# Step 2 of each batch of SSM parameters, moved from one unit behind step 1 to 1.6 units behind, with its TensorE work queued behind that unit's op 7

## The chip, the cores and the metric

The kernel runs on one core of one Trainium2 chip. The metric is the device time of one execution, in microseconds (us). The engines of the core each work through a queue of their own: TensorE (PE, and PEld for its weight loads), VectorE (DVE), ScalarE (ACT), GpSimd (POOL), and SyncE (SP), which here issues all transfers.

## What is computed

One layer of a decoder, for a prompt of 1024 tokens and 8 samples of 4 tokens (1056 columns in all): a SwiGLU feed-forward half, a mixing block (windowed attention beside a diagonal state-space model, the SSM), and a second feed-forward half. Cut to what the change touches:

```python
def swiglu(x, w1, w3, w2):
    return (jax.nn.silu(x @ w1) * (x @ w3)) @ w2

def trunk_layer(x, ...):
    x = x + 0.5 * swiglu(rms_norm(x, p['ffn1_norm']), p['ffn1_w1'], p['ffn1_w3'], p['ffn1_w2'])
    ...
    y_ssm, new_re, new_im = s5_scan(u, s_re, s_im, a_re, a_im, log_dt, b_re, b_im, c_re, c_im, d)
```

`s5_scan` needs, from its parameters alone (not from x), discretised matrices for 32 groups of channels. The kernel works these out in 8 batches of 4 groups, while the first feed-forward half runs.

## The kernel before, in words

The first feed-forward half has 22 blocks of hidden columns (NFF = 22). Blocks 0 and 1 are multiplied plainly; blocks 2 to 21 go through `up`, one **unit** each. A unit makes the products with w1 and w3 by seven block products (a Winograd-like scheme), the **ops**, in the order 4, 3, 1, 2, 5, 7, 6 (`OPS`). An op has 24 matmuls on TensorE: two column halves, four row blocks, and three passes (high x high, high x low, low x high parts of fp32 operands); a unit has 168. All matmuls of products are recorded by one line of the helper `passes` (L197). The results lie in PSUM tiles P (three buffers of two banks); ops 4, 3, 1 and 6 open a new one. ScalarE and VectorE empty them into the tile e: for op 7 an add (L378), a Silu on ScalarE, and a product with op 2's result (L380), after which the tile of ops 4 and 2 is free.

Weights come four transfers to a unit (L292), are combined on VectorE (ws), and split by ScalarE (cast wh, L308) and VectorE (wl) into eight buffers each, so one op more than a unit. Tiles of 1056 columns share a pool T of 34 buffers. In `up`, 28 of them hold the operands X (seven ops, two halves, high and low); e takes one per unit, and each batch of parameters two, ta and tb.

The SSM parameters of a batch come from the generator `params_b`, in two steps divided by its `yield` (L553). **Step 1** loads "bc" into tb (L528), then GpSimd alone computes: bb and ca into tb, ba and e_ into ta (line L80 for all of it). **Step 2** stores e_ (L554), transposes ba on TensorE (four, "ptr", L559), copies the result with ScalarE to mt (L560) and stores it; copies ca and bb to c2 and b2 (L568, L569), reorders c2 to cp (L573); multiplies b2 by c2 on TensorE (eight matmuls "pk", L580); copies that to kt (L583); spreads kt over tz with eight small transfers (L593), casts it to tp (L595) and stores it. The tiles of step 2 share a pool of four buffers, and "ptr" and "pk" share two PSUM banks (sm).

`hook(f)` is called at the end of unit f. For odd f from 5 to 19 it starts step 1 of batch b = (f - 5) / 2; for even f from 6 to 20 it runs step 2. That fixes the order in which the program is traced, not the order in the engines' queues: the framework plans each queue ahead with its own timing model, takes at any moment the instruction that it has as ready, and prefers the one traced earlier. `issue_after(ins)` adds an edge that holds the instructions traced in the block, on the engine of `ins` only, behind `ins` in that engine's queue; the other engines' instructions are held by their data and buffers alone.

After unit 21 the down projection `down` begins: it loads hr (L396), splits it (cast hh on ScalarE, L398), loads w2a, and multiplies into tiles p.

Of the kernel before, what the change touches and what calls it, by code (L numbers as in the profile page):

```python
# [34 lines left out]
NB = 8  # L35
# [7 lines left out]
def body(tc, I, O):  # L43
    nc = tc.nc
    V, S, Pl, PE = nc.vector, nc.scalar, nc.gpsimd, nc.tensor
    dma = nc.sync.dma_start
    mark = {}
    es = ExitStack()
    with es:
# [32 lines left out]
        def mul(o, a, b, e=V):  # L82
            tt(o, a, b, ALU.mult, e)

        def add(o, a, b, e=V):
            tt(o, a, b, ALU.add, e)

        def sub(o, a, b, e=V):
            tt(o, a, b, ALU.subtract, e)
# [10 lines left out]
        def act(o, a, f, **kw):  # L100
            S.activation(o, a, f, **kw)
# [7 lines left out]
        def TT(name, dt=F32):  # L109
            return big(Tp, "T", name, dt)  # L110
# [5 lines left out]
        def SQ(name, dt=F32, w=C):  # L116
            return sq_p.tile([128, H], dt, tag="sq", name=name)[:, 0:w]
# [35 lines left out]
        def load_consts():  # L153
            dma(vec[:, ARE:], I["vec"][:, ARE:])
            dma(ident, I["ident"])
            dma(mask, I["mask"])
            dma(dvec, I["dvec"])
# [35 lines left out]
        def passes(ps, w, x, first, last, **kw):  # L193

            (h, l), (xh, xl) = w, x
            for i, (a, b) in enumerate(((h, xh), (h, xl), (l, xh))):
                PE.matmul(ps, a, b, start=first and i == 0, stop=last and i == 2, **kw)  # L197

        def gemm_to(ps, wks, xs, cols):
            n = len(wks)  # L200
            for k, ((wu, kb), x) in enumerate(zip(wks, xs)):
                passes(ps, blk(wu, kb), [t[:, cols] for t in x], k == 0, k == n - 1)
# [85 lines left out]
        def wload(s1, s3):  # L288
            r1, r3 = (wr_p.tile([128, 8, 128], F32, tag="wr", name="wr") for _ in range(2))
            a11, a12, a21, a22 = r1[:, 0:4], r1[:, 4:8], r3[:, 0:4], r3[:, 4:8]  # L290
            for a_, src in ((a22, s3[:, 4:8]), (a11, s1[:, 0:4]), (a21, s3[:, 0:4]), (a12, s1[:, 4:8])):
                dma(a_, src)  # L292
            return a11, a12, a21, a22

        def wprep(raw):

            a11, a12, a21, a22 = raw
            W = {}
            for op in OPS:
                if op in RAW:  # L300
                    s = a11 if op == 3 else a22
                else:
                    p, q, f, o = {1: (a11, a22, add, None), 5: (a11, a12, add, None), 2: (a21, a22, add, None),
                                  7: (a12, a22, sub, a12), 6: (a21, a11, sub, a21)}[op]
                    s = ws_p.tile([128, 4, 128], F32, tag="ws", name="ws") if o is None else o
                    f(s, p, q)
                h, l = w4()
                S.copy(h, s)  # L308
                sub(l, s, f32(h))
                W[op] = h, l  # L310
            return W
# [3 lines left out]
        def products(W, X, first):  # L315

            P = {}

            def one(op, j):
                b = BANK[op]  # L320
                for k in range(4):
                    passes(P[b][:, j, 0:J], [t[:, k, :] for t in W[op]], [t[:, k, :] for t in X[op, j]],
                           k == 0 and op in OPENS, k == 3, skip_group_check=op not in OPENS)

            both = slice(0, 2)
            if first:
                for op in OPENS[:3]:
                    P[BANK[op]] = bank("pp", f"P{BANK[op]}")
                for j in range(2):
                    for op in OPS[:6]:  # L330
                        one(op, j)
                        yield op, slice(j, j + 1), P[BANK[op]][:, :, 0:J]
                ops = OPS[6:]
            else:
                ops = OPS
            for op in ops:
                if op in OPENS:
                    P[BANK[op]] = bank("pp", f"P{BANK[op]}")
                for j in range(2):
                    one(op, j)  # L340
                yield op, both, P[BANK[op]][:, :, 0:J]

        def plain(f, j, wu, X, hid):

            P = [bank("pp", f"Q{i}") for i in range(2)]
            e = SQ("e", w=H).rearrange("p (b c) -> p b c", b=2)
            for b in range(2):
                for w_, p in zip(wu, P):
                    for k in range(KD):
                        passes(p[:, b, 0:J], blk(w_, k), [t[:, k % 4, :] for t in X[k // 4, b, j]], k == 0, k == KD - 1)  # L350
                act(e[:, b], P[0][:, b, 0:J], AF.Silu)
                mul(e[:, b], e[:, b], P[1][:, b, 0:J])
                yield
            dma(hj(hid[f], j), e)

        def up(w1, w3, X, hid, f0, hook=None):

            for f in range(f0, NFF):
                W = wprep(wload(w1[f], w3[f]))
                e = TT("e")  # L360
                q_, g_ = (e[:, i * H:i * H + H].rearrange("p (j c) -> p j c", j=2) for i in range(2))
                a_ = SQ("a1", w=H).rearrange("p (j c) -> p j c", j=2)
                for op, js, p_ in products(W, X, f == f0):
                    q, g, a1, p = (t[:, js, :] for t in (q_, g_, a_, p_))
                    if op == 4:
                        S.copy(q, p)
                    elif op == 3:
                        add(q, q, p)
                    elif op == 1:
                        add(g, q, p)  # L370
                    elif op == 5:
                        act(a1, p, AF.Silu)
                        sub(q, q, p)
                    elif op == 2:
                        c21 = p_
                        sub(g, g, p)
                    elif op == 7:
                        mark["up"] = V.tensor_tensor(out=q, in0=q, in1=p, op=ALU.add).ins  # L378
                        act(q, q, AF.Silu)
                        mul(q, q, c21[:, js, :])  # L380
                        dma(hid[f, :, 0:H].rearrange("p (j c) -> p j c", j=2)[:, js, :], q)
                    else:
                        add(g, g, p)
                        mul(g, g, a1)
                        mark["hid"] = dma(hid[f, :, H:T], e[:, H:T]).ins
                if hook:
                    hook(f)

        def down(w, hid, xd_, x, groups):

# [206 lines left out]

        todo = []

        def hook(f):  # L600

            if f == 2:
                with tc.issue_after(mark["hid"]):
                    load_consts()
                with tc.issue_after(mark["up"]):
                    params()
            elif 4 < f < 5 + 2 * NB:
                if f % 2:
                    todo.append(params_b((f - 5) // 2))
                next(todo[-1], None)  # L610


        hid = dr.tile([NFF, 128, T], F32, name="hid")
# [27 lines left out]
        def sums(B, b):  # L641
            ps = SM("ss")[:, 0:J]
            for a in range(2):
                for i in range(2):
                    s = SQ("sq", w=H).rearrange("p (k c) -> p k c", k=2)
                    act(s, B[a, b][:, 2 * i:2 * i + 2, :], AF.Square)
                    for kk in range(2):
                        PE.matmul(ps, f32(ones), s[:, kk, :], start=a + i + kk == 0, stop=a == 1 and i + kk == 2)
            return ps
# [14 lines left out]
        ps = sums(B[0], 0)  # L664
# [22 lines left out]
        for _ in cmb:  # L687
            pass
        up(I["w1a"], I["w3a"], X, hid, 2, hook)
        banks(mm=(4, 1), sm=(4, 1))  # L690
        x = []
# [594 lines left out]
        for _ in combos(B[1], X, 1):  # L1286
            pass
        up(I["w1b"], I["w3b"], X, hid, 2)
        banks(mm=(4, 1), sm=(4, 1))
        x = []  # L1290
# [127 lines left out]
```

## Time and profile before

| | us |
|---|---|
| time, median of 3 runs | 2186.34 (2185.17 to 2187.98) |
| the profiled execution, its own time | 2187.48 |
| its span, first to last instruction | 2185.7 |
| TensorE busy | 2097.5 (96%) |
| VectorE busy | 1409.7 (64%) |
| ScalarE busy | 751.6 (34%) |
| GpSimd busy | 368.7 (17%) |

The profile is one execution. Busy time is the time in which an engine has an instruction running; TensorE's matmuls are pipelined, one of 264 columns shows 0.28 us and the next begins 0.12 us after it. A mark such as [1.64 <-POOL ta L80] in a timeline says that the engine was idle for 1.64 us before the instruction, and that a write of ta by GpSimd at line 80 ended the wait. [...]

### The profile page before, as it was taken

What the parts mean: (1) busy time and instruction counts of PE and PEld (TensorE: products, weight loads), DVE (VectorE), ACT (ScalarE), POOL (GpSimd) and SP (SyncE); (2) the same over time, 40 slices, a digit from 0 to 9 for tenths busy, and PEclk for the clock granted to TensorE, in tenths of its full rate; (3) what the DMA queues carried; (4) which work ended last, traced back from release to release, by engine and by line L of the source; (5) the groups of instructions that cost most, each with busy time, mean ns of one, the idle gap of its engine ahead of it and who ended that gap; (6) DMA issues with size and microseconds to landing.
All of it is one profiled execution on the core that took longest, in us unless ns stands there. A gap on an engine that the chain in (4) does not pass through costs nothing.

```text
span 2185.7 us, 38056 instructions
## 1 busy us (share of the span) xinstructions
PE 2097.5 (96%) x15009; PEld 2064.6 (94%) x15009; DVE 1409.7 (64%) x2580; ACT 751.6 (34%) x1435; POOL 368.7 (17%) x759
## 2 busy tenths in 40 slices
PE   7999999999999999999899799988999999999999
PEld 7999998999999999999899699988999999999999
DVE  5876566655554375757988856778666666565534
ACT  5433343434221152235455543344322222332210
POOL 0017777565000032324200200000000000000000
PEclk8999999999999999999999799999999999999999
DMA  4122322333632234642222264331222212273212
GB/s 157 43 93 83 108 95 82 108 100 120 245 133 59 63 118 159 206 123 68 76 84 93 77 241 153 129 104 40 82 66 88 86 64 86 76 248 118 92 38 80
DMA packets 132947, 234.40 MB, mean 107 GB/s; under 512 B 25936, under 2 KB 62608, under 8 KB 132752
## 3 DMA queue, kind: packets, MB, share of 16 engines
q1 hardware_dynamic: 132768, 231.97, 31.9%
q8 instruction: 118, 1.93, 0.4%
q14 instruction: 61, 0.50, 0.1%
HBM read 164.98 MB, written 64.06 MB: 105 GB/s over the span
## 4 chain that ended last, share of the span: by engine, by line
PE 73%; DVE 7%; POOL 3%; issue 2%; DMA 1%; SPq 1%; ACT 1%; DVEq 0%; POOLq 0%; ACTq 0%
PE p L197 26%; PE P L197 26%; PE pj L197 10%; PE pm L197 4%; POOL tb L80 2%; PE Q L197 2%; PE pg L197 1%; DVE raw L80 1%; POOL ta L80 1%; DVE wl L80 1%; SPq L593 1%; PE po L1016 1%; DVE Xl L80 0%; PE pt L1001 0%; PE sc L975 0%
## 5 line engine op out<-in xcount | busy, mean ns | idle before, releaser
L197 PE MATMUL P<-Xh,wh 128*128 128x264 f32 x2240 | 643.2, 287 | 12.2 <-DVE e L80 7.1
L197 PE MATMUL P<-Xl,wh 128*128 128x264 f32 x2240 | 640.8, 286 | 0.0
L197 PE MATMUL P<-Xh,wl 128*128 128x264 f32 x2240 | 638.4, 285 | 0.0
L197 PEld LDWEIGHTS P<-Xh,wh 128*128 128x128 f32 x2240 | 426.4, 190 | 16.9 <-DVE e L80 6.2
L197 PEld LDWEIGHTS P<-Xh,wl 128*128 128x128 f32 x2240 | 426.6, 190 | 0.0
L197 PEld LDWEIGHTS P<-Xl,wh 128*128 128x128 f32 x2240 | 426.1, 190 | 0.0
L197 PE MATMUL p<-hh,wh 128*128 128x352 f32 x1056 | 340.4, 323 | 5.2 <-DVE x L92 3.4
L197 PE MATMUL p<-hh,wl 128*128 128x352 f32 x1056 | 340.5, 322 | 0.0
L197 PE MATMUL p<-hl,wh 128*128 128x352 f32 x1056 | 340.2, 322 | 0.0
L80 DVE TENSOR_TENSOR wl<-wr,wh 128x512 fp32r<-128x512 f32 (+1 forms) x360 | 246.2, 685 | 115.9 <-ACT wh L308 85.8
L92 DVE SCALAR_TENSOR_TENSOR x<-p,x 128x352 f32<-128x352 f32 x288 | 150.3, 523 | 246.8 <-PE p L197 243.7
L185 ACT CAST wh<-wr 128x512 fp32r<-128x512 f32 (+1 forms) x200 | 120.1, 603 | 460.9 <-PE p L197 331.0
L80 DVE TENSOR_TENSOR e<-e,P 128x528 f32<-128x528 f32 (+1 forms) x250 | 169.8, 680 | 158.2 <-PE P L197 128.1
L197 PE MATMUL pj<-xh,wh 128*128 128x352 f32 x624 | 204.3, 327 | 6.5 <-DVE gt L80 5.4
L197 PEld LDWEIGHTS p<-hh,wh 128*128 128x128 f32 x1056 | 198.3, 188 | 6.5 <-DVE x L92 4.3
L197 PE MATMUL pj<-xl,wh 128*128 128x352 f32 x624 | 203.2, 326 | 0.0
L197 PE MATMUL pj<-xh,wl 128*128 128x352 f32 x624 | 202.7, 325 | 0.0
L197 PEld LDWEIGHTS p<-hl,wh 128*128 128x128 f32 x1056 | 198.7, 188 | 0.0
L197 PEld LDWEIGHTS p<-hh,wl 128*128 128x128 f32 x1056 | 198.5, 188 | 0.0
L308 ACT CAST wh<-wr 128x512 fp32r<-128x512 f32 x160 | 99.5, 622 | 266.2 <-PE P L197 225.9
L308 ACT CAST wh<-ws 128x512 fp32r<-128x512 f32 x120 | 74.5, 622 | 208.9 <-PE P L197 203.0
L197 PEld LDWEIGHTS pj<-xh,wh 128*128 128x128 f32 x624 | 118.6, 190 | 7.9 <-DVE gt L80 5.9
(692 smaller groups left out, 3481.8 us busy)
## 6 DMA issues: line engine op xcount, KB each, us to landing
hr<-hid SPq DMA_DIRECT2D x44, 528.0 KB
hid<-e SPq DMA_DIRECT2D x86, 264.0 KB
wr<-in_w_in SPq DMA_DIRECT2D x26, 512.0 KB
wr<-in_w3a SPq DMA_DIRECT2D x40, 256.0 KB
wr<-in_w1a SPq DMA_DIRECT2D x40, 256.0 KB
wr<-in_w2a SPq DMA_DIRECT2D x40, 256.0 KB
wr<-in_w3b SPq DMA_DIRECT2D x40, 256.0 KB
wr<-in_w1b SPq DMA_DIRECT2D x40, 256.0 KB
```

Of the source, the lines that this page charges most:

```text
L80: e.tensor_tensor(out=o, in0=a, in1=b, op=op)
L92: V.scalar_tensor_tensor(out=o, in0=a, scalar=s, in1=b, op0=op0, op1=op1)
L185: S.copy(h[:, 0:m, :], r[:, i:i + m, :])
L197: PE.matmul(ps, a, b, start=first and i == 0, stop=last and i == 2, **kw)
L308: S.copy(h, s)
L593: dma(tv[:, j, :, j * 16:128], ktg[:, :, 0:(8 - j) * 16])
L1016: PE.matmul(po[:, 0:256], Vs[blk // 4][:, blk % 4, m // 2, :], P[:, a_, kb * 256:kb * 256 + 256], start=i == 0, stop=i == 2 * nk - 1)
```

## The change

Step 1 stays at the end of the odd units. Step 2 of a batch is traced no longer at the end of the unit after step 1, but a unit later, inside unit f + 2, right after op 7's results are taken over, and inside an order edge: `mark["pe"]` is the last matmul traced so far, that of op 7, and the TensorE instructions of step 2 (ptr and pk) stand behind it in TensorE's queue. Batch 0 has step 1 at the end of unit 5 and step 2 in unit 7; batch 7 has step 1 at the end of unit 19 and step 2 in unit 21, the last. Within a unit in which both happen, the older batch's step 2 is traced first.

```diff
             for i, (a, b) in enumerate(((h, xh), (h, xl), (l, xh))):
-                PE.matmul(ps, a, b, start=first and i == 0, stop=last and i == 2, **kw)
+                mark["pe"] = PE.matmul(ps, a, b, start=first and i == 0, stop=last and i == 2, **kw).ins
...
                         dma(hid[f, :, 0:H].rearrange("p (j c) -> p j c", j=2)[:, js, :], q)
+                        if hook:
+                            hook(f, False)
...
                 if hook:
-                    hook(f)
+                    hook(f, True)
...
-        def hook(f):
-
+        def hook(f, end):
+
+            if not end:
+                if f > 5 and f % 2:
+                    with tc.issue_after(mark["pe"]):
+                        next(todo.pop(), None)
+                return
             if f == 2:
...
-            elif 4 < f < 5 + 2 * NB:
-                if f % 2:
-                    todo.append(params_b((f - 5) // 2))
-                next(todo[-1], None)
+            elif f > 4 and f % 2 and f < 5 + 2 * NB:
+                todo.append(params_b((f - 5) // 2))
+                next(todo[-1])
```

## Rows read from the trace of the kernel before

**Rows 1.** The page's first part: engine, busy us, share, instructions.

```profile
PE 2097.5 (96%) x15009; PEld 2064.6 (94%) x15009; DVE 1409.7 (64%) x2580; ACT 751.6 (34%) x1435; POOL 368.7 (17%) x759
```

**Rows 2.** Waits of TensorE, 60 to 560 us: line, releaser, total, times, longest.

```profile
PE ptr L559 <- POOL ta L80: 17.5, 12, 2.0
```

**Rows 3.** Timeline of TensorE: start, duration, line, output from inputs, wait.

```profile
265.36 0.83 PE L559 MATMUL ptr<-ident,ta 128*128 128x128 f32 x3
267.82 0.48 PE L559 MATMUL ptr<-ident,ta 128*128 128x128 f32 x1 [1.64 <-POOL ta L80]
267.95 0.57 PE L197 MATMUL P<-Xh,wh 128*128 128x264 f32 x1
...
289.99 0.62 PE L580 MATMUL pk<-c,b 128*16 128x128 f32 x8
```

**Rows 4.** Timeline of GpSimd, batch 2: first, last of ba, last of e_.

```profile
256.49 0.44 POOL L80 TENSOR_TENSOR tb<-tb,par 128x32 f32<-128x32 f32 x2 [11.11 <-issue]
...
267.31 0.45 POOL L80 TENSOR_TENSOR ta<-tb 128x128 f32<-128x128 f32 x1
...
290.56 0.46 POOL L80 TENSOR_TENSOR ta<-tb 128x128 f32<-128x128 f32 x1
```

**Rows 5.** Windows, ptr to next product: length, busy, clock; sum of batches 1-7.

```profile
177.48:177.83 0.35, 0.35 (x6) 0.35 (x5) 0.15 (x1) 0.22 (x1) 0.27 (x2) 1.00 0.64 228
...
354.56:360.21 5.65, 1.05 (x6) 0.43 (x5) 4.47 (x6) 0.99 (x2) 5.18 (x9) 0.98 0.33 107
...
sum 23.83, PE 5.98 PEld 2.80 DVE 14.56 ACT 6.44 POOL 21.69; mean PE 0.85 PEld 0.40 DVE 2.08 ACT 0.92 POOL 3.10
```

**Rows 6.** Windows, the seven units from behind pk to ptr: their sum.

```profile
sum 143.40, PE 143.40 PEld 143.40 DVE 94.53 ACT 50.32 POOL 58.98; mean PE 20.49 PEld 20.49 DVE 13.51 ACT 7.19 POOL 8.43
```

**Rows 7.** Windows, the seven units from behind ptr to pk: two, and sum.

```profile
222.27:244.32 22.05, 22.05 (x169) 21.91 (x169) 12.71 (x18) 9.35 (x23) 19.39 (x52) 0.92 0.19 67
...
313.00:333.52 20.52, 20.52 (x169) 20.38 (x169) 12.33 (x18) 9.24 (x23) 18.10 (x48) 1.00 0.25 78
...
sum 152.32, PE 152.32 PEld 151.35 DVE 83.83 ACT 65.21 POOL 132.88; mean PE 21.76 PEld 21.62 DVE 11.98 ACT 9.32 POOL 18.98
```

**Rows 8.** Timeline of SP, batch 1's tz and batch 2's in_bc.

```profile
251.84 2.49 SPq L593 DMA_DIRECT2D tz<-kt  x4
254.38 0.58 SPq L528 DMA_DIRECT2D tb<-in_bc  x1
```

**Rows 9.** Waits of SP's queue, 60 to 560 us.

```profile
SPq L554 <- POOL ta L80: 109.1, 8, 15.2
```

**Rows 10.** Timeline of TensorE and ScalarE at the seam to the down projection.

```profile
544.93 0.36 PE L197 MATMUL P<-Xh,wh 128*128 128x264 f32 x1 [1.69 <-DVE e L80]
...
548.95 0.40 PE L197 MATMUL p<-hh,wh 128*128 128x352 f32 x1 [0.89 <-DVE e L80]
...
541.20 1.08 ACT L398 CAST hh<-hr 128x1056 fp32r<-128x1056 f32 x1 [3.17 <-DMA hr<-hid]
...
542.70 0.60 ACT L101 ACTIVATE a<-P 128x528 f32<-128x528 f32 x1
```

**Rows 11.** Tiles mt, c2, b2, cp: ns min/median/max, first and last start.

```profile
L560 ACT COPY mt<-ptr x16: 364/372/376, 178.1 to 500.4; 128x256 f32<-128x256 f32 x16
...
L568 ACT COPY c<-tb x32: 428/433/438, 180.9 to 507.0; 64x288 f32<-64x288 f32 x32
...
L569 ACT COPY b<-tb x32: 211/215/219, 181.2 to 505.7; 64x32 f32<-64x32 f32 x32
...
L573 ACT COPY cp<-c x32: 407/414/426, 184.6 to 508.5; 128x128 f32<-128x128 f32 x32
```

**Rows 12.** Timeline of ScalarE and TensorE behind ptr, batches 0 and 2.

```profile
182.50 0.65 ACT L101 ACTIVATE e<-e 128x528 f32<-128x528 f32 x1
...
183.94 0.39 PE L197 MATMUL P<-Xh,wh 128*128 128x264 f32 x1
...
273.90 0.62 ACT L308 CAST wh<-wr 128x512 fp32r<-128x512 f32 x1
```

## Prediction

> **What bounds the kernel now.** The page comes first: TensorE is busy 96% of the span [rows 1]. So only what makes TensorE wait, or lowers its clock, can give time. The change touches the first up-projection alone, about 98 to 543 us, so the waits of that stretch come next. There the largest wait of TensorE is for the transposes "ptr" (L559), and what ends it is GpSimd writing "ta" [rows 2]. The timeline of TensorE shows the place. Each group of four transposes stands in its queue between op 7 and op 6 of a unit. I counted the products: 168, one unit, lie between each ptr group and the eight matmuls "pk" (L580), and 168 again up to the next ptr; the last 24 products, op 6 of unit 21, stand alone at 544.93 us [rows 3, 10]. Of batch 2, three transposes run at 265.36 and the fourth waits until 267.82 [rows 3]. The data it waits for left GpSimd at 267.31 + 0.45 us, in a chain that had begun only at 256.49 and runs on to 291 [rows 4].
>
> So step 1 is too late for step 2, although the program puts step 2 one unit later. Counting units back from the end, ptr of batch b stands behind op 7 of unit 5+2b, ahead of the place where the program traces it (end of unit 6+2b): the planner took it earlier, as soon as it thought it ready. That is the fault the change is aimed at.
>
> **What the waits cost.** I measured the eight stretches from the first transpose of a batch to the next product. Batch 0 did not wait: 0.35 us. Batches 1 to 7 took 23.83 us together [rows 5]. What can go is 23.83 - 7 x 0.35 = 21.4 us. (The waits list has 17.5 us; it leaves out the start-up of a matmul after each wait.)
>
> Behind that comes a second cost. The unit before each ptr group, from pk to ptr, takes 20.49 us at a granted clock of 1.00, in all seven cases, sum 143.40 us [rows 6]. The unit behind each ptr group holds the same 168 products, and the seven of them take 152.32 us. [...] Difference: 8.9 us. Together 30.3 us are there to win, 1.4% of the time.
>
> **The change, part by part.**
> *The record of the last matmul* (L197) adds no instruction: nothing.
> *Step 1* stays at the end of unit 5+2b; it is only traced after the previous batch's step 2 instead of being followed by it. *Step 2* of batch b moves from the end of unit 6+2b to op 7 of unit 7+2b, and its 12 TensorE instructions get an order edge behind the last product of that op 7. ptr so goes two units later in TensorE's queue than it stands now, 2 x 20.49 + 0.9 (ptr and pk) = 41.9 us. It is now at most 5.65 us too early [rows 5], so the data is there some 36 us ahead. The 21.4 us go, and the 8.9 us of low clock with them. What is late next on that data is nothing on TensorE: GpSimd needs 34.5 us for a batch (256.49 to 291.0) [rows 4], against 41.9 us for two units.
>
> *SP's queue.* in_bc, which starts step 1, stands behind eight tz transfers of the batch before [rows 8]; with step 2 later these come a unit further on, so step 1 starts up to 5 us earlier: a gain only for slack. The store of "ta" (L554) is not held by the edge. It waits for GpSimd 109.1 us over the eight batches already [rows 9], and the weight loads behind it wait too; TensorE does not feel it, as the eight wh/wl buffers hold a unit of weights (20.5 us). If two units take 41.9 us instead of 45.7 and GpSimd still 34.5, that cover shrinks by about 4 us. I cost it at nothing; without cover it would be those 4 us per batch.
>
> *ptr and pk themselves* are as many as before: nothing.
>
> *pk's new place* is the unknown. Its operands c2 and b2 are copied by ScalarE out of "tb", and the planner will have it ready shortly after ptr, no longer a unit later. mt copies 2 x 0.37, then 4 x 0.43 and 4 x 0.22 = 2.6 us [rows 11]; with 0.3 us from ptr to the first copy and perhaps a Silu of 0.65, ready 3.6 to 4.3 us after ptr. If pk stands behind op 6, TensorE arrives 0.35 + 24 x 0.122 = 3.3 us after ptr, so it waits 0.3 to 1.1 us; if it stands some products further on, or the copies run before ptr (their data is ready long before), it waits nothing. No case of such a wait is in the trace (pk at 289.99 ran at once [rows 3]). The nearest row is batch 0, where the Silu of op 7 came late behind the copies, at 182.50, and op 3 at 183.94 lost about 0.2 us, with no loss of clock [rows 12]. I take 0.5 us x 8 = 4.0 us; bounds 0 and 1.1 x 8 = 8.8. A gain is excluded, since the pk instructions only ever add their own run.
>
> *Batch 7 at the seam.* Its ptr moves from 497.41 to behind op 7 of unit 21, at 543 us, where the down projection begins and TensorE already waits (1.69 us and 0.89 us), because ScalarE, in its order, sits on the cast hh until the transfer hr has landed [rows 10]. ScalarE gets the whole of step 2 there: the 3.3 us above, 4 cp copies 1.66, and about 1.8 of kt and tp casts, 6.8 us; SP gets the eight tz transfers among the hr loads. Against that, hr loads at 530 us are free of the tz ahead of them, and could shorten the two waits. Bounds: -2 us and +6.8 us. I take +1.5 us, near the small end, since 6.8 us of ScalarE work falls in a stretch where down products of 0.16 us need few casts.
>
> Sum: -21.4 - 8.9 + 4.0 + 1.5 = -24.8 us. The profiled execution took 2187.48 us (span 2185.7 [rows 1]), 1.14 above the median of 2186.34; the difference applied to the median gives **2161.5 us**. With both bounds of the last two terms the forecast reaches from 2154.0 (-32.3) to 2171.6 (-14.7).
>
> **Rivals.**
> *A: ScalarE's order makes pk wait longer.* If one or two weight casts stand between the copies, the last copy ends 0.6 to 1.3 us later, and pk waits some 1.7 us. Such a wait did cost low clock in five of seven cases and not in two [rows 7], so 0.8 us on top: 2.5 x 8 = 20. -30.3 + 20 + 1.5 = -8.8: 2177.5 us. For it: in batch 2 a cast (273.90) does stand between copies [rows 12]. Against it: step 2 would be traced ahead of the next unit's casts. [...]
> *B: slower.* The planner has the copies done before ptr or much faster than the chip, and puts pk directly behind ptr, ahead of op 6, while on the chip the copies come after. TensorE then waits 0.3 + 0.74 + 2.6 = 3.6 us, and with the 1.56 us of low clock (22.05 - 20.49 [rows 6, 7]) that is 5.2 x 8 = 41.6: -30.3 + 41.6 + 1.5 = +12.8, 2199.1 us. It decides from (30.3 - 1.5) / 8 = 3.6 us a batch. For it: ptr today is just such a misjudgement of the planner. Against: it needs a gap ahead of op 6 in the plan that the chip doesn't have, of over 3 us.
> *C: the wait is of another kind, and stays.* If step 1 is late for want of a T buffer, holding ta and tb a unit longer makes it later still: X takes 28 of 34 buffers, e two, two batches of ta and tb the last four. Then nothing is gained: 2186.34 + 1.5 = 2187.8 us. Against: what ends the wait is GpSimd's own work, after a start that SP's queue delayed [rows 4, 8], and four buffers are what two batches need. [...]
>
> **How the numbers follow.** Forecast 0.73, A 0.12, B 0.10, C 0.05. About 0.2% (4.4 us) is what a measurement of this kernel can tell from no change. Faster by more: the forecast and three quarters of A (0.09), 0.82. Within: the rest of A and C, 0.08. Slower: B, 0.10. Range for 8 in 10: the forecast's with a little room below for a better seam, and A with room for longer waits: 2152 to 2184.
>
> **What would show it.** In the profile after: no wait of ptr for GpSimd; ptr two units later behind GpSimd's last "ta" of its batch; every unit from the first ptr to the seam 20.5 us at a clock of 1.00, so that the stretch from 177 us to the last unit's op 7 shrinks by some 26 to 30 us. Wrong, if pk (L580) shows up among TensorE's waits with ScalarE as releaser at over 1.1 us each, if weights (wh or wl) end TensorE's waits, or if the two waits at the seam grow by over 7 us.

## The result and the profile after

The changed kernel takes 2174.92 us (median; 2172.84 to 2177.64) beside 2186.26 for the kernel before: a ratio of 0.9948, 95% interval 0.9931 to 0.9965, so 11.3 us less. Run again beside later experiments it gave 2173.75 us, ratio 0.9949 (0.9933 to 0.9966). The forecast was 24.8 us less, with 2154.0 to 2171.6 us between the bounds of its terms; the result lies above that, though inside the wider range of 2152 to 2184, which the rival A had opened. TensorE is busy for 96% of the span, as before [rows 1].

First TensorE's waits from 60 to 560 us in the changed kernel (line, releaser, total, times, longest), then those of SP's queue and of VectorE in the same stretch:

```profile
PE P L197 <- DVE e L80: 8.6, 9, 2.1
PE pk L582 <- ACT b L571: 1.0, 2, 0.5
...
SPq L556 <- POOL ta L80: 124.6, 8, 17.6
...
DVE ws L80 <- DMA wr<-in_w1a: 21.2, 5, 5.0
```

The wait of ptr for GpSimd [rows 2] is gone altogether. In its place products of the up-projection wait for VectorE's "e". The store of e_ (now L556), which already stood 109.1 us at the head of SP's queue [rows 9], stands there 124.6 us. VectorE waits 21.2 us for weights (w1a); in the kernel before it was 0.4 us, once.

The timeline of TensorE in the changed kernel shows ptr on time and the new wait right behind it, in batch 3, and the wait of batch 4 (start, duration, line, output from inputs, wait):

```profile
346.69 0.60 PE L561 MATMUL ptr<-ident,ta 128*128 128x128 f32 x4
348.75 0.36 PE L197 MATMUL P<-Xh,wh 128*128 128x264 f32 x1 [1.46 <-DVE e L80]
...
393.68 0.36 PE L197 MATMUL P<-Xh,wh 128*128 128x264 f32 x1 [2.06 <-DVE e L80]
```

All four transposes run at once, where batch 2's were torn in two [rows 3]. The product behind them is the first of op 6. It needs a PSUM buffer, and the line at 347.92 of the chain below is the subtraction by which VectorE empties that of op 5: it ends at 347.92 + 0.69 = 348.61, and op 6 starts at 348.75. This comes in batches 3 to 7: 1.46, 2.06, 0.76, 1.89 and 0.69 us, 6.9 together. Batches 0 to 2 do not have it. The second profile of the same kernel shows it too, in batches 3 to 6 (1.05, 1.05, 1.44 and 2.77 us; all waits of TensorE for e from 60 to 560 us):

```profile
PE P L197 <- DVE e L80: 7.8, 8, 2.8
```

In the first profile the starts of ptr say the same: 218.53, 261.17, 303.81, 346.69, 391.02, 437.49, 481.15 and 526.57 us. Two units take 42.64 us at first, then 42.9 to 46.5. I had expected 41.9 throughout.

The chain behind the wait, in batch 3: SP's queue, VectorE and GpSimd in the changed kernel.

```profile
334.27 0.46 POOL L80 TENSOR_TENSOR ta<-tb 128x128 f32<-128x128 f32 x1
...
334.75 0.33 SPq L556 DMA_DIRECT2D pb_d<-ta  x1
335.17 0.38 SPq L598 DMA_DIRECT2D pb_d<-tp  x1
335.64 0.89 SPq L292 DMA_DIRECT2D wr<-in_w3a  x2
336.63 0.89 SPq L292 DMA_DIRECT2D wr<-in_w1a  x2
...
338.51 0.48 SPq L530 DMA_DIRECT2D tb<-in_bc  x1
...
341.25 0.69 DVE L80 TENSOR_TENSOR ws<-wr 128x512 f32<-128x512 f32 x1 [4.62 <-DMA wr<-in_w1a]
...
347.92 0.69 DVE L80 TENSOR_TENSOR e<-e,P 128x528 f32<-128x528 f32 x1
```

GpSimd's last write of e_ starts at 334.27. SP's store goes at 334.75, and all that stood behind it follows in one burst: another store, four weight loads, two stores of hidden columns, and at 338.51 in_bc, the load that starts the next batch's step 1 [rows 8]. VectorE gets w1a so late that it idles 4.62 us, and what stands behind that instruction runs late, down to the subtraction at 347.92; so op 6 waits. The load in_bc closes a loop: it stands behind a store that waits for GpSimd, and GpSimd's next batch waits for it (timeline of GpSimd, start of two batches, as in [rows 4]; the profile names in_bc for seven of the eight starts):

```profile
254.04 1.47 POOL L80 TENSOR_TENSOR tb<-tb,par 128x32 f32<-128x32 f32 x2 [9.72 <-DMA tb<-in_bc]
...
300.15 0.45 POOL L80 TENSOR_TENSOR tb<-tb,par 128x32 f32<-128x32 f32 x2 [10.59 <-DMA tb<-in_bc]
```

GpSimd's batches start at 165.3, 209.6, 254.0, 300.1, 345.1, 388.2, 433.4 and 478.1 us, 44.7 us apart on the mean: some 35 of work and some 10 of waiting. TensorE, at 42.64 us for two units, is now quicker than this loop. It gains about 2 us on it in each batch, and from batch 3 on it has caught up.

Two smaller costs. "pk" used to stand in one place; it now stands in two, half in each (TensorE, batch 0 in the changed kernel):

```profile
222.98 0.28 PE L197 MATMUL P<-Xh,wh 128*128 128x264 f32 x1
223.19 0.61 PE L582 MATMUL pk<-c,b 128*16 128x128 f32 x4
223.73 0.39 PE L197 MATMUL P<-Xl,wh 128*128 128x264 f32 x1
223.96 0.29 PE L197 MATMUL P<-Xh,wl 128*128 128x264 f32 x1
...
224.89 0.61 PE L582 MATMUL pk<-c,b 128*16 128x128 f32 x4
```

From the product ahead (222.98) to the second one behind (223.96) are 0.98 us, where two products alone take 2 x 0.122. So a place costs 0.74 us. In the kernel before, the one place with all eight matmuls [rows 3] cost as much: from the product ahead (289.78) to the second one behind (290.76) are 0.98 us too. The second place is what the change pays, 0.7 us a batch, without a wait.

And the seam to the down projection, first TensorE's timeline there in the changed kernel:

```profile
527.87 0.36 PE L197 MATMUL P<-Xh,wh 128*128 128x264 f32 x1 [0.69 <-DVE e L80]
531.48 0.61 PE L582 MATMUL pk<-c,b 128*16 128x128 f32 x4 [0.48 <-ACT b L571]
532.61 0.61 PE L582 MATMUL pk<-c,b 128*16 128x128 f32 x4 [0.52 <-ACT b L571]
534.11 0.40 PE L197 MATMUL p<-hh,wh 128*128 128x352 f32 x1 [0.89 <-DVE dd L80]
```

Then the first 20 us of the down stage, as windows (length, busy of PE with its count, PEld, DVE, ACT, POOL, granted TensorE clock as a share of the full one, DMA share, GB/s), in the changed kernel and, in the second fence, in the kernel before:

```profile
534.10:554.10 20.00, 19.99 (x115) 20.00 (x116) 9.11 (x17) 5.38 (x12) 1.36 (x6) 0.91 0.85 290
```

```profile
548.95:568.95 20.00, 19.41 (x119) 19.12 (x120) 8.77 (x15) 3.92 (x5) 0.00 (x0) 1.00 0.93 349
```

Op 7 of unit 21 ends 16.5 us earlier than before (526.6 against 543.0), the first down product comes 14.8 us earlier (534.11 against 548.95 [rows 10]), and the first product of the stage behind it 12.8 us earlier (795.9 against 808.7). So 3.7 us of the gain are given back at the seam: 1.7 ahead of the down stage, 2.0 in it, where the granted clock is 0.91 for 20 us instead of 1.00. Of the 1.7 us, 1.1 are only batch 7's own ptr and pk (0.35 and 0.74 us), which in the kernel before ran ahead of this op 7. So the seam itself costs 2.6 us in this execution.

In the second profile of the same kernel it costs nothing. From batch 7's ptr to the first down product are 5.57 us there against 7.54 here, pk waits for nothing, and the clock stays up (the first 20 us of its down stage):

```profile
530.61:550.61 20.00, 20.00 (x124) 20.00 (x125) 9.73 (x18) 5.48 (x12) 1.36 (x6) 1.00 0.83 291
```

### The profile page after: what moved, and what is told of

Read it like the earlier page. It is cut to its first block, busy times and chain, and to the rows that moved or that the text cites. A ratio compares the mean times of both kernels' runs of the same rounds, so it can differ in the third digit from the quotient of the medians.

```text
span 2175.9 us, 38065 instructions
## 1 busy us (share of the span) xinstructions
PE 2097.8 (96%) x15009; PEld 2064.3 (95%) x15009; DVE 1411.8 (65%) x2580; ACT 748.1 (34%) x1435; POOL 370.3 (17%) x759
```

## The experiments

My theory, **S**: the store of e_ blocks SP's queue until GpSimd is done, and so makes weights and the next in_bc late. Against it **A**, the rival of the prediction: ScalarE's copies of step 2 stand ahead of casts and Silus, and VectorE waits for those. **G**: GpSimd's work itself, too long for two units.

The change touches the stretch from the first unit to the first down product. This table has the profiled executions of all kernels by stretch, in us; the first and the last column show that executions also differ, by up to 2 and 4 us, in stretches that no edit is aimed at.

| | ahead of the first unit | first unit to first down product | down stage | behind it |
|---|---|---|---|---|
| before | 91.0 | 457.9 | 259.8 | 1377.0 |
| the changed kernel | 91.2 | 442.9 | 261.8 | 1380.0 |
| the changed kernel, second profile | 90.1 | 440.6 | 260.3 | 1379.5 |
| experiment 1 | 91.1 | 431.0 | 259.9 | 1380.3 |
| experiment 2 | 90.3 | 436.2 | 265.4 | 1376.8 |
| experiment 3 | 89.8 | 427.9 | 260.4 | 1377.3 |
| experiment 4 | 89.2 | 430.4 | 259.6 | 1378.2 |
| experiment 5 | 91.2 | 428.5 | 269.2 | 1376.5 |
| experiment 6 | 90.4 | 462.7 | 260.4 | 1377.7 |

**1. The store waits behind op 7.** In the changed kernel the store gets an order edge behind the store of op 7's hidden columns, so that it reaches SP's queue when GpSimd is long done.

```diff
-            dma(pb_d[b, :, 512:1024], ta[:, 512:1024])
+            with tc.issue_after(mark["q"]):    # q: op 7's store to hid
+                dma(pb_d[b, :, 512:1024], ta[:, 512:1024])
```

> The changed kernel, with the store of e_ (pb_d from ta) held in SP's queue behind the transfer of op 7's result of step 2's own unit. Theory S (SP's queue): the store waits for GpSimd at the head of SP's queue (124.6 us over eight batches), the weight loads behind it come late, VectorE's ws waits for them (21.2 us, up to 5.0), empties op 5 late, and op 6 behind ptr waits for its PSUM buffer in batches 3 to 7 (1.46, 2.06, 0.76, 1.88, 0.69 us, with 1.6 us of low clock behind the longest). Then these waits go: from ptr to ptr 42.6 us in every batch, about 9 us less than the changed kernel, near 2166 us. Theory A (ScalarE's order): the copies of step 2 ahead of op 7's Silu make VectorE late. Then the waits stay and the time is that of the changed kernel, about 2175 us.

Measured: 2163.9 us, ratio to the kernel before 0.9907 (0.9892 to 0.9921). TensorE's waits from 60 to 560 us:

```profile
PE P L197 <- DVE e L80: 1.4, 3, 0.5
```

The waits of op 6 fall from 8.6 to 1.4 us, no wait for GpSimd is among SP's seven largest any more (the seventh is 14.2 us; it was 124.6 us), none for w1a among VectorE's seven (the seventh is 4.9 us; it was 21.2 us), and ptr comes every 42.64 to 42.71 us in all batches. GpSimd is idle 6 to 9 us between batches instead of about 10. The ScalarE copies stand behind ptr and ahead of op 7's Silu as they did: A falls. So does G, since GpSimd does the same work. The edge frees two things at once, the weight loads and in_bc, so what each of them is worth stays open.

**2. The same edge alone, in the kernel before.** Nothing else is changed there.

```diff
-            dma(pb_d[b, :, 512:1024], ta[:, 512:1024])
+            with tc.issue_after(mark["hid"]):
+                dma(pb_d[b, :, 512:1024], ta[:, 512:1024])
```

> The kernel before, with the same store held in SP's queue behind the transfer of op 6's result of the unit that ended last. Nothing else of the change. Theory S says that the order of ptr in TensorE's queue and the late start of step 1 stay, so ptr waits for GpSimd as before: 2183 to 2188 us. Rival: SP's blocked queue was what made step 1 late already in the kernel before, so ptr waits less: near 2170 us.

Measured: 2176.1 us, ratio 0.9958 (0.9944 to 0.9973). The time lies between my expectation and the rival's. TensorE's largest waits:

```profile
PE ptr L560 <- POOL ta L80: 8.5, 7, 1.6
PE p L197 <- DVE x L92: 4.7, 1, 4.7
```

The wait of ptr falls from 17.5 us [rows 2] to 8.5, and from batch 1 on ptr comes every 42.8 to 44.1 us instead of every 43.5 to 49.6. So in the kernel before, too, the blocked queue was part of the reason that GpSimd came late. One edge on a store gave 9 us there, nearly what the whole change gives. In the profiled execution, the quickest of the four at 2170.47 us, the stretch that the change touches even falls by 21.7 us (457.9 to 436.2); 5.6 of them are lost in the down stage, where p waits 4.7 us for x. So there most of the 30.3 us of the prediction went without moving step 2.

**3. pk in one place.** Experiment 1, with a third step: pk, kt and tz are divided from ptr, mt and the copies, and go behind op 7 of the next unit.

```diff
             ...                                # copies c2, b2, cp
+            yield
             ...                                # pk, kt, tz, tp
...
-                if f > 5 and f % 2:
+                if f > 6:
+                    b = (f - 7) // 2
                     with tc.issue_after(mark["pe"]):
-                        next(todo.pop(), None)
+                        next(todo[b], None)
+                        if f == NFF - 1:
+                            next(todo[b], None)
```

> As the run with the store held behind op 7, and the part of step 2 from kt on (pk and all behind it) made a third step, held in TensorE's queue behind op 7 of the unit after (batch 7's stays with its step 2). In the changed kernel pk stands at two places, two matmuls each, and each place takes 0.54 us and 0.09 us of gap, against 0.55 and 0.09 for the four together in the kernel before. If an interruption of the products has a price of its own, two units take 42.0 instead of 42.6 us: 0.65 x 7 = 4.5 us less than the run with the store held, near 2161 us. If the price is that of the matmuls themselves, the time is the same as that run's.

Measured: 2156.34 us, ratio 0.9872 (0.9856 to 0.9888), 7.6 us below experiment 1. TensorE, batch 1:

```profile
279.44 0.28 PE L197 MATMUL P<-Xh,wl 128*128 128x264 f32 x1
279.65 0.62 PE L584 MATMUL pk<-c,b 128*16 128x128 f32 x8
280.20 0.39 PE L197 MATMUL P<-Xh,wh 128*128 128x264 f32 x1
```

pk is in one place, and ptr comes every 41.93 to 41.99 us: the 41.9 us of the prediction, all through. From the first ptr to the last are 293.71 us against 298.68 in experiment 1, 5.0 less, which is what the split was to cost. About 2 us of that are lost again ahead of the first down product, which waits longer than there (0.95 us in experiment 1):

```profile
517.71 0.40 PE L197 MATMUL p<-hh,wh 128*128 128x352 f32 x1 [2.24 <-DVE e L80]
```

So the stretch shrinks by 3.1 us; the rest of the 7.6 us lies ahead of the first unit and behind the first down product, and is not explained here. This is the quickest kernel of the study.

**4. GpSimd's work cut.** The changed kernel without the loop that computes e_.

```diff
-            for m in range(7):
-                ...                            # cmul
+            Pl.memset(e_, 1.0)
```

> The changed kernel, with the loop that fills e_ left out (seven rounds of six GpSimd operations; one memset in its place), so that GpSimd needs about 17.5 us for a batch instead of 34.5. The transfers and their order in the program are the same. Theory S: the store finds GpSimd done, SP's queue doesn't stand, the waits of op 6 go, about 2166 us. Theory A: no difference, about 2175 us.

Measured: 2159.55 us, ratio 0.9887 (0.9873 to 0.9902). The waits of op 6 go here too, and ptr comes every 42.64 to 42.70 us. TensorE's waits from 60 to 560 us:

```profile
PE P L197 <- DVE e L80: 1.4, 3, 0.5
```

The time is 6 us under the 2166 that S expected and 4.3 under experiment 1, but the stretch that the change touches is only 0.7 us shorter than there. With GpSimd quick, the store is where it was, and no wait for GpSimd is among SP's seven largest (the seventh is 13.5 us, beside 124.6 us for the store in the changed kernel); with GpSimd slow and the store held (experiment 1), there is none either. It takes both, the long work and the store in front of the loads.

**5. The last batch a unit earlier.** Experiment 3, with batch 7's step 2 behind unit 20 and its step 3 behind unit 21; in all batches the store of e_ goes at the start of step 3.

```diff
-            with tc.issue_after(mark["q"]):
-                dma(pb_d[b, :, 512:1024], ta[:, 512:1024])
             ...                                # step 2
             yield
+            with tc.issue_after(mark["q"]):
+                dma(pb_d[b, :, 512:1024], ta[:, 512:1024])
...
-                        if f == NFF - 1:
-                            next(todo[b], None)
+                        if f == NFF - 2:
+                            next(todo[NB - 1])
```

> As the kernel with pk in a third step and the store held back (2156.3 us beside a before of 2183.4, ratio 0.9872), but batch 7's step 2 is issued behind unit 20's products and its step 3 behind unit 21's, one unit earlier than there; and in every batch the store of e_'s row is issued at the start of step 3. This measures the seam term. If the last batch's place at the seam costs time (my theory: about 2 to 4 us there), the waits of op 6 and of the first p for VectorE's e around the seam shrink, the first down product comes 2 to 4 us sooner, and the ratio is about 0.986 (2153). If the seam's loss is that of the down stage's own clock or of VectorE's remaining work whatever the place, the ratio stays at 0.987 (2155 to 2158). If batch 7's GpSimd loop is not done by unit 20 (it starts about when unit 20 does, 35 us long), TensorE waits for it and the time is 5 to 15 us above 2156.

Measured: 2167.27 us, ratio 0.992 (0.9905 to 0.9934), 11 us above experiment 3. The number is that of the third expectation, but not its mechanism: no ptr waits for GpSimd. Up to the seam nothing is lost (ptr every 41.93 us). At the seam (SP's queue, ScalarE, then TensorE):

```profile
517.43 0.39 SPq L579 DMA_DIRECT2D pb_d<-ta  x1
...
522.39 0.53 SPq L387 DMA_DIRECT2D hid<-e  x1
522.96 0.43 SPq L398 DMA_DIRECT2D hr<-hid  x1
...
526.78 3.21 SPq L406 DMA_DIRECT2D x<-in_x  x5
...
523.66 1.09 ACT L599 COPY tp<-tz 128x512 f32<-128x512 f32 x1 [5.46 <-DMA tz<-kt]
526.89 1.07 ACT L400 CAST hh<-hr 128x1056 fp32r<-128x1056 f32 x1 [2.14 <-DMA hr<-hid]
...
519.74 0.40 PE L197 MATMUL p<-hh,wh 128*128 128x352 f32 x1 [3.66 <-DVE e L80]
...
535.13 0.66 PE L197 MATMUL p<-hh,wh 128*128 128x352 f32 x1 [4.28 <-DVE x L92]
```

Eight tz transfers, one at 516.17 and seven from 517.87 to 522.3 us, lie ahead of the last store of hidden columns, the load hr and the loads of x. ScalarE idles 5.46 us on tz with hh behind it, but hh has to wait for hr after that as well, 2.14 us. TensorE waits 3.66 us for the last add of the up-projection and 4.28 us for x, and the granted clock from 520 to 540 us is 0.77. In experiment 3 the last store of hidden columns and the first load of x go ahead of the tz transfers (518.51 and 518.97 us). The kernels differ in two things here, the last batch's place and the store's, so what each is worth stays open; that the down stage can take 9 us longer (269.2 against 260.4) when its loads stand behind the tz transfers in SP's queue is seen. What the seam of the changed kernel costs in one execution and not in the other, this run does not settle.

**6. The third step without holding the store.** The changed kernel with experiment 3's third step, the store where the change has it.

```diff
             dma(pb_d[b, :, 512:1024], ta[:, 512:1024])   # as in the change
             ...                                # copies c2, b2, cp
+            yield
             ...                                # pk, kt, tz, tp
```

> The changed kernel with pk and kt alone moved to a third step, behind op 7 of the next unit; the store of e_'s row stays where the change has it, at the head of SP's queue right behind e_'s loop. If the costs add (pk split in two places about 0.65 us a batch, the store's loop by itself about 9 us), it gains 8 x 0.6 = 4.9 us on the changed kernel: 2170 beside a before of 2183.4 (ratio 0.9939 against 0.9948 there is then 0.9925). My theory says that the loop of GpSimd, SP's store, the loads behind it and the next batch's step 1 is the bound of batches 3 to 7 at about 44.7 us each, so that TensorE, made 0.65 us a batch quicker, only uses up its cover sooner and waits longer in op 6: the gain is 0 to 2 us (2171 to 2175 by the ratio of the changed kernel), with the waits of op 6 for VectorE's e at 10 to 13 us instead of 7 to 8.6.

Measured: 2193.5 us, ratio 1.0042 (1.0028 to 1.0055): slower than the kernel before. Both expectations missed. TensorE's, SP's and ScalarE's waits from 60 to 560 us:

```profile
PE P L197 <- DVE e L80: 27.7, 10, 7.2
SPq L556 <- POOL ta L80: 164.0, 8, 23.6
ACT tp L598 <- DMA tz<-kt: 44.0, 7, 10.0
```

The place of the largest, batch 2, in the timelines of SP, ScalarE, VectorE and TensorE:

```profile
291.62 0.32 SPq L556 DMA_DIRECT2D pb_d<-ta  x1
292.03 2.47 SPq L292 DMA_DIRECT2D wr<-in_w3a  x2
294.60 0.38 SPq L292 DMA_DIRECT2D wr<-in_w1a  x1
295.07 0.54 SPq L596 DMA_DIRECT2D tz<-kt  x1
...
302.12 1.09 ACT L598 COPY tp<-tz 128x512 f32<-128x512 f32 x1 [10.00 <-DMA tz<-kt]
...
303.76 0.69 DVE L80 TENSOR_TENSOR wl<-ws,wh 128x512 fp32r<-128x512 f32 x1 [3.80 <-ACT wh L308]
...
310.80 0.56 PE L197 MATMUL P<-Xh,wh 128*128 128x264 f32 x1 [7.17 <-DVE e L80]
```

It is theory S over again, by a second road. The tz transfers of batch b now stand behind the store of batch b+1, which waits for GpSimd. The copy tp waits for tz on ScalarE, 10.00 us, and the weight casts wh behind it start only at 303.12; VectorE waits for wh, and op 6 waits 7.17 us for VectorE. Between this kernel and experiment 3 the place of one store is the only difference (with its edge): 37 us of medians, 1.7%.

## Why the prediction was wrong

**Right: the 30.3 us were there.** ptr's wait is gone, and the low clock behind it with it in batches 1 to 3: in the kernel before, five of the seven units behind a ptr group (batches 1, 2, 4, 6 and 7) show a granted clock of 0.88 to 0.93 and take 21.98 to 23.10 us, the two others show 1.00 and take 20.52 and 20.57 us [rows 7]; in the changed kernel the windows behind ptr of batches 1 to 3 show 1.00. Once the two other costs are out of the way (experiment 3) two units take 41.93 us, the stretch is 30.0 us shorter than before (427.9 against 457.9), and the gain is 28.0 us by ratio (1.28% of 2186). The reason given for them was right only in part. The prediction laid them to ptr's place in TensorE's queue; experiment 2 left ptr where it was, and in its profile 21.7 us of the stretch went with SP's queue freed.

**Wrong: SP's queue "at nothing".** This is the step that failed. The prediction saw the store wait for 109.1 us [rows 9], said that the cover would shrink by about 4 us a batch, and put it at zero because eight wh/wl buffers hold a unit of weights. Two things in that step were wrong. The cover was counted at TensorE, but the first engine to run out was VectorE, idle for w1a up to 5.0 us while its adds, which free PSUM buffers, stood behind. And the load in_bc stands behind the same store, so that GpSimd's period is its work and the trip through SP's queue, 44.7 us and not 34.5. The right comparison was that period against 41.9 us; the row of before had both parts of it, 11.11 us idle ahead of 34.5 us of work [rows 4]. The price: from the first to the last ptr of the changed kernel are 308.04 us, and seven times 42.64 are 298.48, so 9.6 us. One of these waits brought low clock back (windows from one ptr group to the next; 1.00 behind the 1.46 us wait, 0.96 behind the 2.06 us one):

```profile
346.80:391.00 44.20, 42.74 (x349) 41.78 (x348) 28.55 (x43) 17.75 (x37) 32.03 (x77) 1.00 0.32 102
391.10:437.40 46.30, 44.24 (x349) 43.28 (x348) 29.66 (x46) 17.85 (x37) 32.33 (x76) 0.96 0.31 97
```

Experiment 1 takes the store away from there and gets about 9 us back by ratio. So the stretch up to the last unit's op 7 shrank by 16.5 us and not by the 26 to 30 that the prediction named as its sign.

**Right size by luck, wrong reason: pk's new place.** I took 4.0 us, as a wait for ScalarE's copies. In batches 0 to 6 pk waits for nothing; the planner set it in two places, and 0.7 us a batch are the price of interrupting the products once more, 5.0 us to batch 6. The bounds (0 to 8.8) held it, but the idea that only a wait can cost was wrong.

**Open: the seam.** 1.5 us were taken, with bounds from -2 to +6.8. The first profile shows 2.6: pk's two waits for ScalarE's copies, 1.0 us in all, are what the prediction had in mind; the clock of 0.91 in the first 20 us of the down stage was not thought of. The second profile has neither, and its seam is 0.9 us shorter than that of the kernel before. What makes the difference stays open.

Put together for the first profile: -30.3 + 9.6 + 5.0 + 2.6 + 3.0 = -10.1, beside -9.8 of its span. The last term lies behind the down stage, at which no edit is aimed and where the prediction had nothing; its cause is open. For the second profile: -30.3 + 9.4 + 5.0 - 0.9 + 2.5 - 1.0 (ahead of the first unit) = -15.3, as its span has it. The gain of the medians, 11.3 us, lies between.

**The rivals.** A predicted a gain of 8.8 us, close to the measured one, but not by what happened: the waits of pk on ScalarE are 1.0 us in two places, not 2.5 us in eight. B did not come: pk stands 34 products behind ptr. C fell: with ta and tb held longer the wait of ptr went, so buffers were not short. In experiments 1 and 3 the gaps go too (ptr every 42.64 to 42.71 and 41.93 to 41.99 us), while the buffers stay as they are. A copy that waits on ScalarE with casts behind it, as A had it, is in the trace of experiment 6: tp idle 10.00 us for tz, starting at 302.12, and the cast wh behind it at 303.12.

The text had named "if weights (wh or wl) end TensorE's waits" as a sign that it was wrong. The releaser that the profile names is "e", one engine's queue further on; only VectorE's waits for w1a lead back to the weights.

## What to carry to other kernels

In this kernel a store that waited for a slow engine, at the head of a queue that also carries loads (124.6 us in the changed kernel, 164.0 us in experiment 6), made that engine's time everyone's. So before speeding up the consumer, read the period of the whole loop (work, store, the loads behind it, the next start) and compare it with the new period of the bottleneck. Cover is to be counted at each engine between the load and the bottleneck, not at the bottleneck alone. And when a step is moved, see what its own transfers now stand behind: the same three steps were 28 us quicker than the kernel before with one store held back, and 9 us slower with it in front. Differences of a few us between two kernels are to be looked for in the stretch that was changed: here some of them lay elsewhere.

## What the runs showed that was not expected

A group of small matmuls that interrupts the stream of products costs about 0.74 us whether it holds half of pk's matmuls or all of them (0.98 us from product to product in both, against 0.24 without it): the number of its matmuls did not matter here, and two places cost twice (ptr every 42.64 us with two, 41.93 us with one).

The granted clock did not fall with every wait of op 6 in the changed kernel: in its two profiles it is 0.96 from one ptr group to the next behind the waits of 2.06 and 2.77 us, and 1.00 behind those of 1.05, 1.44, 1.46 and 1.89 us.
